# The first stage of a two-block transformer kernel: modulation by native fp32 products in column quarters, the norm's multiplications on another engine, five projections by parts, and filler products

## The chip, the cores and the metric

The kernel runs on one core of a Trainium2 chip. The metric is the device time of one execution in microseconds, the median of several executions. Lower is better. All work is in fp32; the inputs lie in the chip's memory when the clock starts.

## The reference, cut to what matters

Two transformer blocks over 512 tokens of 1024 channels run one after the other. The change lies in the first lines of block 1:

```python
m = silu(c) @ w_mod + b_mod                  # c: 1 x 1024, w_mod: 1024 x 6144
sh1, sc1, g1, sh2, sc2, g2 = split(m, 6)
mc = silu(c_ctx) @ w_mod + b_mod             # the same weights for the context
h = rms_norm(x, norm1_g) * (1 + sc1) + sh1       # x: 512 tokens x 1024
hc = rms_norm(ctx, norm1_g) * (1 + csc1) + csh1  # ctx: 256 tokens x 1024
# four mixers on h @ w_in and hc @ w_in: grouped attention, neighbourhood
# attention, a Fourier mix, and a 31-tap convolution; gates, w_out, experts
```

`rms_norm` divides each token by the root of the mean square over its 1024 channels. Nothing of `h @ w_in` can start before the shifts and scales of the modulation (`sh1`, `sc1`) and the norm of `x` are there.

## The kernel before, in words

All tensors lie transposed, channels on the partitions and tokens along the free axis: `x` is 8 chunks of 128 channels by 512 tokens. A product in fp32 is made of three products in a reduced fp32 type (`mm3`): each operand is split into a high and a low part (`h_hi`, `h_lo`; `whi`, `wlo`), and high times high, low times high and high times low are added up in a PSUM bank. The high part of a weight is a CAST on ScalarE (ACT), the low part a subtraction on VectorE (DVE). A weight that is not split is multiplied natively in fp32 (called whole in `_load`).

The program is written as threads (generators). While it is built, a rough clock of the engines (class `Clock`) picks which thread is traced next, and each engine then runs its instructions strictly in the traced order. Every instruction passes through the helper `Lane.call`, so nearly all rows of the profile carry line L320; instructions are told apart by their tiles. Weights come in loads of 512 KB on SP's queue (SyncE); a load waits until its tile in a ring is free, and what stands behind it on SP waits too.

The first stage (`mixers`) is:

- `silu_c` (line 706) makes silu of `c` and `c_ctx` (tile `csil`) and its split (`cparts`).
- `modulated` (771) makes the squares of `x` on ACT (`xsq`), adds the eight chunks on DVE (`xacc`), sums over the channels by four products of TensorE (PE) with ones, takes the power -0.5 on GpSimd (POOL, `xr`), spreads the result by four transposes, copies it out of PSUM (`xbc`) and multiplies the eight chunks of `x` by it on POOL.
- `jobs_mod` (727) and `mod_job` (734) make the modulation's 2048 columns for `sh1` and `sc1` in four groups of 512 columns: four loads of `w_mod` each (`mraw`), the first one native, the other three split (`mod_hi`, `mod_lo`). A product has 4 columns of `csil` or `cparts` as its stationary side and 512 columns of the weights as its moving side, so its result stands on 4 partitions. The group's sum is copied to SBUF (`m`), turned to the partitions by four small products (`pairs`), and gives a shift and a scale `A` for two chunks of `x`, the event `mod0` to `mod3`.
- `modulated_chunk` (791) makes `h_hi` and `h_lo` of one chunk from these, on ACT and DVE.
- `conv_first` (1010) multiplies the first 3 (`FIRST`) units of `w_in` at once, by pairs of chunks: as soon as a pair of chunks of `h` is there, 3 units by 6 products run. The convolution has 8 such units; `conv_job` does the others one after the other, 24 products each. `taps` then makes the 31 taps of four channel groups on DVE; a group needs two units.
- `zeros` clears a row in memory (`yg`) by DMA from a tile `ct` that POOL clears. On SP's queue these DMAs stand ahead of the tables of the Fourier mix (`ldft`).
- The context goes through `modulated` too (`hcsq`, `hcacc`, `hcr`, `ctx`), beside the first units.

Of the kernel before, what the change touches and what calls it, by code (L numbers as in the profile page):

```python
# [35 lines left out]
FIRST = 3  # L36
# [71 lines left out]
_HALF = np.concatenate([np.arange(0, 64, 2), np.arange(1, 64, 2)])  # L108

# the columns of w_mod by 128: shift and scale of each 256 channels, and the rest  # L110
# [92 lines left out]
def _span(ap):  # L203
    """the tile of an access pattern, and the range of its elements on a partition"""
    pairs = ap.ap
    row = pairs[0][0]
    lo = ap.offset % row if row > 0 else ap.offset
    hi = lo
    for s, n in pairs[1:]:
        d = s * (n - 1)  # L210
        if d < 0:
            lo += d
        else:
            hi += d
    return ap.tensor.name, lo, hi + 1


class Clock:
# [91 lines left out]
class Lane:  # L310
    """an engine, with what is traced on it noted on the clock"""
# [26 lines left out]
class Ring:  # L338
    """tiles that are taken and given back in any order"""
# [17 lines left out]

class Thread:
# [9 lines left out]
class Net:  # L368
    """The kernel. What it does is written as threads (generators), which yield the engine that their next
    instructions run on and what those wait for; `run` traces them in the order of a rough clock's times, the first  # L370
    in time first. Each engine runs its instructions in the order in which they are traced."""
# [199 lines left out]
    def proj(self, out, w, act, kt, n):  # L571
        """out[128 channels, n tokens] = the weights' columns by the activations"""
# [5 lines left out]
    def proj_t(self, out, w, act, t):  # L578
        """out[128 tokens of tile t, 256 channels]; w: the two halves of the contraction"""
# [7 lines left out]
    def split(self, hi, lo, src, *free):  # L587
        """hi + lo = src; then the rings' tiles in `free` are given back"""
# [7 lines left out]
    def evacuate(self, out, p, n):  # L596
        """a bank's first n columns into out"""
# [8 lines left out]
    def evacuated(self, ring, p, n):  # L606
        """a bank's first n columns, in a tile of the ring"""
# [8 lines left out]
    def rsqrt_mean(self, out, sums, n):  # L616
        """out = (sums / n + eps) ** -0.5"""
# [6 lines left out]
    def row_bcast(self, out_sb, colv, nt):  # L624
        """out_sb[128, nt * 128] = the [128 tokens, nt] column values, along the tokens on every row"""
# [8 lines left out]
    def square(self, acc, x, sq, first, scaled=None):  # L634
        """acc (+)= x ** 2, by a tile of the ring sq; scaled: also (f * x) ** 2, by f and its square"""
# [15 lines left out]
    def column_sums(self, r, acc, nt, n):  # L651
        """r[128 tokens, nt] = (mean over n channels of the squares in acc + eps) ** -0.5"""
# [7 lines left out]
    def sumsq(self, p, nt, k, x, sq):  # L660
        """columns of p: the sums over the 128 channels of chunk k of x ** 2, by tokens"""
        yield ACT, x, sq
        t = sq.take()
        self.nc.scalar.activation(t[:, :nt * 128], x, AF.Square)
# [6 lines left out]
    def rms(self, r, p, nt, nk):  # L671
        """r[128 tokens, nt] = (mean over the chunks' channels + eps) ** -0.5; the bank p is given back"""
# [6 lines left out]
    def square_last(self, x, sq, event):  # L679
        """a tile of the ring sq with x ** 2"""  # L680
# [6 lines left out]
    def column_sums2(self, r, acc, x, sq, event, nt, n):  # L687
        """r[128 tokens, nt] = (mean over n channels of the squares in acc, and of those of x, which the event gives,
        + eps) ** -0.5"""
# [16 lines left out]
    def silu_c(self):  # L706
        """silu(c) and silu(c_ctx), and their parts"""
        nc = self.nc
        self.csil = self.keep.tile([128, 8, 4], F32, name="csil")
        nc.gpsimd.memset(self.csil, 0.0)  # L710
        self.cparts = self.keep.tile([128, 8, 4], F32R, name="cparts")
        self.pairs = self.keep.tile([4, 2], F32, name="pairs")
# [5 lines left out]
        c = self.csil[:, :, :2]  # L718
# [4 lines left out]
        nc.vector.tensor_tensor(self.pairs, self.ident[:4, :2], self.ident[:4, 2:4], op=OP.add)  # L723
        yield from self.split(self.cparts[:, :, 0:2], self.cparts[:, :, 2:4], c)
        self.mark("cparts", self.cparts, c)

    def jobs_mod(self, a, after=None):
        if after:
            yield [], partial(self.hold, after)
        for g in range(2 * a, 2 * a + 2):  # L730
            for kq in range(4):
                yield [(self.T["wmod1"][g, kq], 2, 512, kq == 0)], partial(self.mod_job, g, kq)

    def mod_job(self, g, kq, w):
        """rows of the bank: the parts of c by the weights' columns"""
        nc = self.nc
        if kq == 0:
            yield PE, self.banks, "cparts"
            self.modp = self.banks.take()
        p = self.modp  # L740
        for k in range(2):
            for z, v in enumerate(w):
                c = self.csil if len(w) == 1 else self.cparts
                nc.tensor.matmul(p[:4, :], c[:, kq * 2 + k], v[:, k], start=kq + k + z == 0,
                                 stop=(kq, k, z) == (3, 1, len(w) - 1))
# [5 lines left out]
        nc.vector.tensor_copy(m, p[:4, :])  # L751
# [2424 lines left out]
```

## Time and profile before

| quantity | before |
|---|---|
| device time, three runs | 2464.28, 2461.07, 2462.39 us |
| median | 2462.39 us |
| span of the profiled execution | 2460.7 us |
| PE busy (products) | 2395.9 us, 97% |
| DVE busy | 1675.1 us, 68% |
| ACT busy | 1236.0 us, 50% |
| POOL busy | 160.3 us, 7% |
| idle time of PE | 64.8 us |

The profile lists the span of the profiled execution; its device time is not listed apart from those of the three runs. The span lies 1.7 us under their median. PE is the engine that sets the time nearly everywhere: of the 64.8 us in which it is idle, 11.3 are its wait for the first load of `w_mod` and 6.0 more fall into the first 50 us. The stage is read from the rows of its engines.

### The profile page before, as it was taken

Reading aid. Unit: us, or ns where it says so; the run is one execution under the profiler, and the core shown is the slowest. Engines: PE = TensorE matmul, PEld = TensorE weight load, DVE = VectorE, ACT = ScalarE, POOL = GpSimd, SP = SyncE. Lnnn points to the kernel's source line nnn. Section 1 sums busy time; section 2 is a strip of 40 time slices with the busy share of each in tenths; the row PEclk is TensorE's granted clock in tenths of the full one; section 3 lists DMA queues with packets and bytes.
Section 4 is the critical chain, followed back from the end, with each engine's and each line's share of the span. In section 5 each row is a group of like instructions: output and inputs, shape, how many; then the busy total and the mean of one; then the engine's idle time right before and its main releaser. Section 6 shows DMA issues by size and latency. Waiting matters only on the chain.

```text
span 2460.7 us, 33539 instructions
## 1 busy us (share of the span) xinstructions
PE 2395.9 (97%) x12332; PEld 2011.6 (82%) x12332; DVE 1675.1 (68%) x3144; ACT 1236.0 (50%) x2135; POOL 160.3 (7%) x179
## 2 busy tenths in 40 slices
PE   7999999999997999999999999999999999999998
PEld 3789788889886788887889888888888888888886
DVE  6997577788455989898998753444569976533443
ACT  4433466468342777775537743332443665432333
POOL 3100122100001110002000000000000000000000
PEclk9999999999997999999999999999999999999999
DMA  6223443521363998985121132222232112222221
GB/s 251 97 69 107 134 128 111 170 77 44 99 213 113 351 384 325 353 325 182 64 78 53 44 103 94 94 97 101 95 101 78 53 64 72 95 100 95 94 98 57
DMA packets 104907, 323.79 MB, mean 132 GB/s; under 512 B 12850, under 2 KB 19922, under 8 KB 104612
## 3 DMA queue, kind: packets, MB, share of 16 engines
q1 hardware_dynamic: 91284, 285.40, 33.0%
q0 software_dynamic: 8560, 25.01, 3.5%
q10 hardware_dynamic: 4896, 11.22, 1.2%
q8 instruction: 98, 1.61, 0.3%
q14 instruction: 69, 0.57, 0.1%
HBM read 308.45 MB, written 13.11 MB: 131 GB/s over the span
## 4 chain that ended last, share of the span: by engine, by line
PE 38%; issue 14%; DVE 1%; DMA 0%; ACT 0%; ACTq 0%; POOLq 0%; POOL 0%; DVEq 0%
PE bank L320 38%; DMA mraw<-yg,dest 0%; DVE wlo L320 0%; DVE G L320 0%; DVE cP L320 0%; DVE ym L320 0%; DVE mt L320 0%; DVE m L320 0%; ACTq L320 0%; DVE x L320 0%; DVE o L320 0%; ACT whi L320 0%; POOLq L3172 0%; POOL r L320 0%; DVE nm L320 0%
## 5 line engine op out<-in xcount | busy, mean ns | idle before, releaser
L320 ACT CAST whi<-wraw 128x1024 fp32r<-128x1024 f32 (+1 forms) x321 | 322.1, 1006 | 666.8 <-PE bank L320 633.2
L320 DVE TENSOR_TENSOR wlo<-wraw,whi 128x1024 fp32r<-128x1024 f32 (+1 forms) x321 | 375.4, 1173 | 155.6 <-ACT whi L320 154.8
L320 PE MATMUL bank<-g_hi,whi 128*128 128x512 f32 x992 | 395.9, 399 | 0.0
L320 PE MATMUL bank<-g_hi,wlo 128*128 128x512 f32 x992 | 387.3, 390 | 0.2
L320 PE MATMUL bank<-g_lo,whi 128*128 128x512 f32 x992 | 386.5, 390 | 0.0
L320 PEld LDWEIGHTS bank<-g_hi,wlo 128*128 128x128 f32 x992 | 186.2, 188 | 40.9 <-DVE wlo L320 1.1
L320 PE MATMUL bank<-h_hi,whi 128*128 128x512 f32 x528 | 216.9, 411 | 1.5 <-ACT whi L320 1.5
L320 PEld LDWEIGHTS bank<-g_hi,whi 128*128 128x128 f32 x992 | 186.5, 188 | 37.9 <-issue 1.9
L320 PEld LDWEIGHTS bank<-g_lo,whi 128*128 128x128 f32 x992 | 186.5, 188 | 37.1 <-issue 1.9
L320 PE MATMUL bank<-h_hi,wlo 128*128 128x512 f32 x528 | 209.3, 396 | 1.3 <-DVE wlo L320 1.3
L320 PE MATMUL bank<-h_lo,whi 128*128 128x512 f32 x528 | 208.6, 395 | 1.6 <-DVE h_lo L320 1.6
L320 PE MATMUL bank<-u_hi,whi 128*128 128x512 f32 x512 | 202.4, 395 | 0.0
L320 PE MATMUL bank<-u_hi,wlo 128*128 128x512 f32 x512 | 200.7, 392 | 0.0
L320 PE MATMUL bank<-u_lo,whi 128*128 128x512 f32 x512 | 198.8, 388 | 0.0
L320 DVE SCALAR_TENSOR_TENSOR mu<-bank,rbc 128x512 f32<-128x512 f32 x64 | 44.0, 691 | 161.0 <-PE bank L320 157.4
L320 ACT CAST whi<-mraw 128x1024 fp32r<-128x1024 f32 x101 | 105.7, 1050 | 55.0 <-PE bank L320 25.1
L320 DVE TENSOR_TENSOR wlo<-mraw,whi 128x1024 fp32r<-128x1024 f32 x101 | 121.0, 1218 | 16.5 <-ACT whi L320 14.5
L320 PEld LDWEIGHTS bank<-h_hi,wlo 128*128 128x128 f32 x528 | 100.6, 191 | 24.5 <-DVE wlo L320 2.5
L320 PEld LDWEIGHTS bank<-h_hi,whi 128*128 128x128 f32 x528 | 101.0, 191 | 21.3 <-ACT whi L320 1.9
L320 PEld LDWEIGHTS bank<-h_lo,whi 128*128 128x128 f32 x528 | 100.9, 191 | 19.5 <-DVE h_lo L320 2.1
L320 PEld LDWEIGHTS bank<-u_hi,wlo 128*128 128x128 f32 x512 | 96.1, 188 | 22.5
L320 PEld LDWEIGHTS bank<-u_lo,whi 128*128 128x128 f32 x512 | 96.1, 188 | 21.2
(539 smaller groups left out, 5017.7 us busy)
## 6 DMA issues: line engine op xcount, KB each, us to landing
mraw<-in_wgu SPq DMA_DIRECT2D x106, 512.0 KB
wraw<-in_win SPq DMA_DIRECT2D x102, 512.0 KB
wraw<-in_wdn SPq DMA_DIRECT2D x78, 512.0 KB
wraw<-in_wup SPq DMA_DIRECT2D x64, 512.0 KB
mraw<-in_wdn SPq DMA_DIRECT2D x50, 512.0 KB
mw<-in_wmod SPq DMA_DIRECT2D x64, 256.0 KB
wraw<-in_wout SPq DMA_DIRECT2D x24, 512.0 KB
wraw<-in_wgu SPq DMA_DIRECT2D x22, 512.0 KB
```

The lines of the kernel that those rows point to most:

```text
L320: r = f(*args, **kw)
```

## The change

The diff, without comments, cut to its core:

```diff
-FIRST = 3
+FIRST = 5
+class Both(Ring):
...
     def sumsq(self, p, nt, k, x, sq):
-        yield ACT, x, sq
+        e = self.lighter()
+        yield e, x, sq
         t = sq.take()
-        self.nc.scalar.activation(t[:, :nt * 128], x, AF.Square)
+        if e == ACT:
+            self.nc.scalar.activation(t[:, :nt * 128], x, AF.Square)
+        else:
+            self.nc.vector.tensor_tensor(t[:, :nt * 128], x, x, op=OP.mult)
         yield PE, t
         for j in range(nt):
             c = j * 8 + k
             self.nc.tensor.matmul(p[:, c:c + 1], t[:, j * 128:(j + 1) * 128], self.ones1, start=True, stop=True)
...
     def silu_c(self):
-        self.csil = self.keep.tile([128, 8, 4], F32, name="csil")
+        self.csil = self.keep.tile([128, 46], F32, name="csil")
-        self.cparts = self.keep.tile([128, 8, 4], F32R, name="cparts")
-        self.pairs = self.keep.tile([4, 2], F32, name="pairs")
+        self.pairs = self.keep.tile([128, 2], F32, name="pairs")
...
+    def warm(self):
+        yield PE, self.banks, self.ident
+        p = self.banks.take()
+        while "x7" not in self.events:
+            yield PE, self.ident
+            self.nc.tensor.matmul(p[:, :128], self.ident, self.ident, start=True, stop=True)
+        self.banks.drop(p)
-    def jobs_mod(self, a, after=None):
+    def jobs_mod(self, groups):
-                yield [(self.T["wmod1"][g, kq], 2, 512, kq == 0)], partial(self.mod_job, g, kq)
+                yield [(self.T["wmod1"][g, kq], 2, 512, True)], partial(self.mod_job, g, kq)
     def mod_job(self, g, kq, w):
         for k in range(2):
-            for z, v in enumerate(w):
-                c = self.csil if len(w) == 1 else self.cparts
-                nc.tensor.matmul(p[:4, :], c[:, kq * 2 + k], v[:, k], start=kq + k + z == 0,
-                                 stop=(kq, k, z) == (3, 1, len(w) - 1))
+            c = 2 * kq + k
+            q = 32 * (c % 4)
+            nc.tensor.matmul(p[q:q + 32, :], self.csil[:, 2 * c:2 * c + 32], w[0][:, k], start=c < 4, stop=c >= 4)
...
-        nc.vector.tensor_copy(m, p[:4, :])
+        nc.vector.tensor_copy(m, p)
...
     def modulated(self, pool, x, nt, v, hi, lo, name):
-        sq = self.ring(pool, 2, [128, n], F32, name + "sq")
-        acc = pool.tile([128, n], F32, name=name + "acc")
+        sq = self.ring(pool, 3, [128, n], F32, name + "sq")
+        yield PE, self.banks, x[:, 0]
+        p = self.banks.take()
         for k in range(8):
-            yield from self.square(acc, x[:, k], sq, k == 0)
+            yield from self.sumsq(p, nt, k, x[:, k], sq)
         r = self.keep.tile([128, nt], F32, name=name + "r")
-        yield from self.column_sums(r, acc, nt, 1024)
-        bc = pool.tile([128, n], F32, name=name + "bc")
-        yield from self.row_bcast(bc, r, nt)
-        for k in range(8):
-            yield POOL, bc
-            nc.gpsimd.tensor_tensor(x[:, k], x[:, k], bc, op=OP.mult)
+        yield from self.rms(r, p, nt, 8)
+        yield PE, self.banks, r
+        bc = self.banks.take()
+        for j in range(nt):
+            nc.tensor.transpose(bc[:, j * 128:(j + 1) * 128], r[:, j:j + 1].to_broadcast([128, 128]), self.ident)
         for k in range(8):
+            yield DVE, bc
+            nc.vector.tensor_tensor(x[:, k], x[:, k], bc[:, :n], op=OP.mult)
             self.spawn(self.modulated_chunk(k, x[:, k], v, hi[:, k], lo[:, k], f"{name}{k}"), 1, name)
...
     def mixers(self):
-            rings = self.ring(pool, 6, [128, 1024], F32, "mraw1"), self.pair_ring(pool, 3, [128, 1024], "mod1")
-            self.m512 = self.ring(pool, 2, [4, 512], F32, "m512")
+            raws = self.ring(pool, 6, [128, 1024], F32, "mraw1")
+            self.m512 = self.ring(pool, 2, [128, 512], F32, "m512")
...
-            self.stream(self.jobs_mod(0), 6, "mod_a", rings, prio=0)
-            self.stream(self.jobs0(), 2, "jobs0")
-            self.stream(self.jobs_mod(1, "jobs0 loaded"), 6, "mod_b", rings, prio=0)
+            self.spawn(self.warm(), 3, "warm", 0.3)
+            firsts = Both(self.pair_ring(pool, FIRST - 3, [128, 1024], "first"), self.his)
+            self.stream(self.jobs_mod((0,)), 8, "mod_a", (raws, None), prio=0)
+            self.stream(self.jobs0(), 2, "jobs0", (self.raws, firsts))
+            self.stream(self.jobs_mod((1, 2, 3)), 8, "mod_b", (raws, None), prio=0)
...
     def jobs0(self):
-        yield [], partial(self.hold, "mod_a loaded")
```

A modulation product now has 32 columns on its stationary side and writes one of the four quarters of a bank's partitions, by the chunk of the contraction; the small products with `pairs` add up the quarters as they turn them. All 16 loads of `w_mod` are taken natively, so the 12 CASTs and 12 subtractions of their splits go. The squares of `x` are made by ACT and DVE, whichever is lighter, and each chunk is summed over its channels by PE at once; the eight multiplications of `x` (and of `ctx`) are done by DVE straight from the PSUM bank. Five units of `w_in` (their parts in two rings that `Both` joins) are loaded ahead and multiplied by pairs of chunks. `warm` puts products of the identity with itself into PE's order wherever the rough clock sees PE idle, until the last chunk of `h` is there.

The traced order changes in the program's first part alone: with buffer numbers left out, PE's order is the same again behind about its first 970 instructions, DVE's behind its first 290 or so. The first place is PE ahead of the first product of `h`. (`bank` is a PSUM bank, `m` the copied sum of a group, `pairs` the small turning products, `ident` the filler.) Before, after the products of groups 0 and 1:

```order
L320 MATMUL bank_69<-mod_hi_138,cparts 4x512
L320 MATMUL bank_69<-mod_lo_141,cparts 4x512
L320 MATMUL bank_71<-pairs,m_143 128x2 x4
L320 MATMUL bank_72<-mraw_132,csil 4x512 x2
L320 MATMUL bank_73<-h_hi,whi_101 128x512
L320 MATMUL bank_73<-h_lo,whi_101 128x512
```

Now, from the last loads of group 3 on:

```order
L320 MATMUL bank_72<-mraw_132,csil 32x512 x2
L320 MATMUL bank_72<-mraw_133,csil 32x512 x2
L320 MATMUL bank_73<-pairs,m_136 128x2 x4
L320 MATMUL bank_67<-pairs,m_137 128x2 x4
L320 MATMUL bank_66<-ident 128x128 x5
L320 MATMUL bank_69<-pairs,m_136 128x2 x4
L320 MATMUL bank_66<-ident 128x128 x29
L320 MATMUL bank_68<-pairs,m_137 128x2 x4
L320 MATMUL bank_66<-ident 128x128 x13
L320 MATMUL bank_70<-h_hi,first_hi_161 128x512
```

The turning products of all four groups, those of group 0 too, moved behind the last product of group 3, 47 fillers stand among and behind them, and the first product of `h` moved behind all of these. From there on 120 products of five units follow, with the context's sums (16 products with ones) and its 2 transposes among them.

The second place is PE's start, which before began with the first load of `w_mod`. Now it begins with 16 fillers, and ends so, down to the first product of group 0 (`xsq` are squares of `x`, each summed by four products with ones):

```order
L320 MATMUL bank_67<-ones_82,xsq_160 128x1 x4
L320 MATMUL bank_66<-ident 128x128 x3
L320 MATMUL bank_67<-ones_82,xsq_158 128x1 x4
L320 MATMUL bank_67<-ones_82,xsq_159 128x1 x4
L320 MATMUL bank_66<-ident 128x128
L320 MATMUL bank_68<-mraw_130,csil 32x512 x2
```

In all 32 products with ones and 27 fillers (16, 3, 4, 3 and 1) now stand ahead of group 0's products; before, four products with ones stood behind the first of them. Another 20 fillers stand between the products of groups 0 and 1.

The third place is POOL. Before:

```order
L320 TENSOR_TENSOR xr<-ms,half 128x4
L320 TENSOR_TENSOR x<-x,xbc 128x512 x8
L320 DMA token<-in_k_token 128x4
L320 TENSOR_TENSOR hcr<-ms,half 128x2
L320 TENSOR_TENSOR ctx<-ctx,hcbc 128x256 x8
L320 MEMSET ct_147 1x512
```

Now:

```order
L320 TENSOR_TENSOR xr<-ms,half 128x4
L320 DMA token<-in_k_token 128x4
L320 TENSOR_TENSOR hcr<-ms,half 128x2
L320 MEMSET ct_142 1x512
```

The clearing of `ct`, for which SP's queue waits, no longer stands behind the eight multiplications of `ctx`.

## Rows read from the trace of the kernel before

**Rows 1.** The page: span, and busy time, share and instructions of each engine.

```profile
span 2460.7 us, 33539 instructions
PE 2395.9 (97%) x12332; PEld 2011.6 (82%) x12332; DVE 1675.1 (68%) x3144; ACT 1236.0 (50%) x2135; POOL 160.3 (7%) x179
```

**Rows 2.** Busy time by stretch (start:end, length, then each engine's), clock, DMA share, GB/s.

```profile
8.00:30.00 22.00, 16.11 (x52) 5.91 (x52) 16.12 (x18) 14.90 (x20) 11.22 (x7) 1.00 1.00 399
...
100.00:150.00 50.00, 50.00 (x288) 44.16 (x287) 46.33 (x80) 19.20 (x40) 0.00 (x0) 0.98 0.16 53
```

**Rows 3.** Timeline of PE (start, duration, instruction, idle time before): modulation, and the first unit.

```profile
11.26 3.57 PE L320 MATMUL bank<-mraw,csil 128*4 128x512 f32 x4 [11.26 <-DMA mraw<-in_wmod]
14.76 1.87 PE L320 MATMUL bank<-ones,xacc 128*128 128x1 f32 x8
21.85 1.88 PE L320 MATMUL bank<-mraw,csil 128*4 128x512 f32 x4
...
35.34 0.80 PE L320 MATMUL bank<-h_hi,whi 128*128 128x512 f32 x1
...
52.84 1.05 PE L320 MATMUL bank<-pairs,m 4*128 4x2 f32 x8
53.82 0.50 PE L320 MATMUL bank<-h_hi,whi 128*128 128x512 f32 x1
```

**Rows 4.** Timeline of PE: products of `h`, the context's sums, the 120th product of `h`.

```profile
63.80 0.39 PE L320 MATMUL bank<-h_hi,wlo 128*128 128x512 f32 x1
...
66.97 0.39 PE L320 MATMUL bank<-h_lo,whi 128*128 128x512 f32 x1
...
71.83 0.50 PE L320 MATMUL bank<-ones,hcacc 128*128 128x1 f32 x4
72.19 0.49 PE L320 MATMUL bank<-h_hi,whi 128*128 128x512 f32 x1
...
78.67 0.39 PE L320 MATMUL bank<-h_hi,wlo 128*128 128x512 f32 x1
```

**Rows 5.** Timelines of DVE and ACT: from the scale of group 2 to the last chunk.

```profile
54.13 0.16 DVE L320 SCALAR_TENSOR_TENSOR A<-mod,vecs 128x4 f32<-128x4 f32 x1
54.39 0.81 ACT L320 ACTIVATE h_hi<-x,mod,A 128x512 fp32r<-128x512 f32 x1 [5.30 <-DVE A L320]
56.88 0.81 ACT L320 ACTIVATE h_hi<-x,mod,A 128x512 fp32r<-128x512 f32 x1 [0.32 <-DVE A L320]
58.31 1.47 DVE L320 TENSOR_TENSOR h_lo<-x,h_hi 128x512 fp32r<-128x512 f32 x2
```

**Rows 6.** Timeline of POOL, and of SP's queue (time of issue).

```profile
20.73 15.97 POOL L320 TENSOR_TENSOR x<-x,xbc 128x512 f32<-128x512 f32 x8 [1.87 <-ACT xbc L320]
74.83 8.78 POOL L320 TENSOR_TENSOR ctx<-ctx,hcbc 128x256 f32<-128x256 f32 x8 [1.07 <-ACT hcbc L320]
83.56 0.52 POOL L320 MEMSET ct<- 1x512 f32 x1
84.11 0.57 SPq L320 DMA_DIRECT2D yg<-ct  x2
...
91.31 9.05 SPq L320 DMA_DIRECT2D wraw<-in_win  x6
```

**Rows 7.** Timeline of PE about the first unit of the Fourier mix.

```profile
94.99 0.39 PE L320 MATMUL bank<-h_hi,wlo 128*128 128x512 f32 x1
96.89 0.50 PE L320 MATMUL bank<-h_hi,whi 128*128 128x512 f32 x1 [1.51 <-ACT whi L320]
...
102.01 0.40 PE L320 MATMUL bank<-h_hi,whi 128*128 128x512 f32 x1
```

**Rows 8.** Groups on DVE (xcount, busy us, mean ns), 68.5 to 87.4 us, then 87.4 to 220.

```profile
L320 DVE SCALAR_TENSOR_TENSOR ca<-cz,vecs,ca 128x512 f32<-128x512 f32 x7 | 7.4, 1087 | 0.0
...
L320 DVE SCALAR_TENSOR_TENSOR ca<-cz,vecs,ca 128x512 f32<-128x512 f32 x113 | 78.8, 745 | 0.5
```

**Rows 9.** A group on DVE, 0 to 60 us.

```profile
L320 DVE TENSOR_TENSOR mod_lo<-mraw,mod_hi 128x1024 fp32r<-128x1024 f32 x12 | 15.9, 1354 | 2.4 <-ACT mod_hi L320 2.4
```

More of the change, by code (lines that the diff above doesn't have):

```diff
@@ L355, in ready, with __init__, take, drop @@
         return free[n - 1] + 0.15 if len(free) >= n else None
+class Both(Ring):
+    def __init__(self, *rings):
+        self.rings = rings
+    def take(self):
+        return min((r for r in self.rings if r.ready() is not None), key=lambda r: r.ready()).take()
+    def drop(self, *tiles):
+        for t in tiles:
+            next(r for r in self.rings if t.tensor.name in r.busy).drop(t)
+    def ready(self, n=1):
+        return min((r.ready() for r in self.rings if r.ready() is not None), default=None)
 class Thread:
@@ L717, in silu_c @@
         yield ACT, cv
-        c = self.csil[:, :, :2]
+        c = self.csil[:, :16].rearrange("p (k c) -> p k c", k=8)
         nc.scalar.activation(c, cv, AF.Tanh, scale=0.5)
@@ L722, in silu_c @@
         nc.vector.tensor_scalar(c, c, 0.5, None, op0=OP.mult)
-        nc.vector.tensor_tensor(self.pairs, self.ident[:4, :2], self.ident[:4, 2:4], op=OP.add)
-        yield from self.split(self.cparts[:, :, 0:2], self.cparts[:, :, 2:4], c)
-        self.mark("cparts", self.cparts, c)
-    def jobs_mod(self, a, after=None):
-        if after:
-            yield [], partial(self.hold, after)
-        for g in range(2 * a, 2 * a + 2):
+        nc.vector.tensor_reduce(self.pairs, self.ident.rearrange("p (q v) -> p v q", q=4)[:, :2], axis=AX.X, op=OP.add)
+        self.mark("csil", c, self.pairs)
+    def warm(self):
[6 more added lines that the diff above has]
+    def jobs_mod(self, groups):
+        for g in groups:
             for kq in range(4):
-                yield [(self.T["wmod1"][g, kq], 2, 512, kq == 0)], partial(self.mod_job, g, kq)
+                yield [(self.T["wmod1"][g, kq], 2, 512, True)], partial(self.mod_job, g, kq)
     def mod_job(self, g, kq, w):
@@ L737, in mod_job @@
         if kq == 0:
-            yield PE, self.banks, "cparts"
+            yield PE, self.banks, "csil"
             self.modp = self.banks.take()
@@ L774, in modulated @@
         n = nt * 128
-        sq = self.ring(pool, 2, [128, n], F32, name + "sq")
-        acc = pool.tile([128, n], F32, name=name + "acc")
+        sq = self.ring(pool, 3, [128, n], F32, name + "sq")
+        yield PE, self.banks, x[:, 0]
+        p = self.banks.take()
         for k in range(8):
-            yield from self.square(acc, x[:, k], sq, k == 0)
+            yield from self.sumsq(p, nt, k, x[:, k], sq)
         r = self.keep.tile([128, nt], F32, name=name + "r")
-        yield from self.column_sums(r, acc, nt, 1024)
-        bc = pool.tile([128, n], F32, name=name + "bc")
-        yield from self.row_bcast(bc, r, nt)
+        yield from self.rms(r, p, nt, 8)
[3 more added lines that the diff above has]
+            nc.tensor.transpose(bc[:, j * 128:(j + 1) * 128], r[:, j:j + 1].to_broadcast([128, 128]), self.ident)
         for k in range(8):
-            yield POOL, bc
-            nc.gpsimd.tensor_tensor(x[:, k], x[:, k], bc, op=OP.mult)
-        for k in range(8):
+            yield DVE, bc
+            nc.vector.tensor_tensor(x[:, k], x[:, k], bc[:, :n], op=OP.mult)
             self.spawn(self.modulated_chunk(k, x[:, k], v, hi[:, k], lo[:, k], f"{name}{k}"), 1, name)
+        self.banks.drop(bc)
         yield DVE, *(f"{name}{k}" for k in range(8))
@@ L819, in modulation_rest @@
                     yield DVE, w
-                    c = self.csil[:, k, 0:1]
+                    c = self.csil[:, 2 * k:2 * k + 1]
                     if k == 0:
```

## The prediction

> **What bounds the kernel now.** I read the page first, then the first 220 us by stretches, then the timelines of PE, DVE, ACT, POOL and SP's queue. PE is busy 2395.9 of 2460.7 us [rows 1], so a change counts where it moves PE's order or opens or closes one of its waits. The new order differs from the old one in the first part alone, and PE has no idle time from 100 to 150 us [rows 2], where DVE is busy for 46.33 of 50 too. So what the first hundred microseconds lose or gain is carried on to the end nearly unchanged, and I price that stretch. Two marks fix it before: the first product of `h` starts at 35.34 [rows 3], and the 120th, which is five units of 24, ends at 78.67 plus one interval of 0.227, at 78.9 [rows 4]. The interval comes from the 15 products from 63.80 to 66.97, 3.17 us for 14 intervals. Behind them PE stands still once more: from 94.99 to 102.01 only ten products start, which at 0.227 take 2.27 of 7.02 us, so 4.75 are lost [rows 7].
>
> **PE's start.** Before, PE begins with the first load at 11.26 and makes four sums. Now 32 sums and 27 fillers stand ahead of group 0. Four sums took 1.87 us at 14.76 [rows 3], 0.47 each; two took 0.36 at 71.83 [rows 4], 0.18 each. A native product of 512 columns is two records: two of them took 3.57 us at 11.26 and 1.88 at 21.85 [rows 3], which are the clock's levels of 1.2 and 2.4 GHz, near 1.75 and 0.9 us a product. A filler of 128 columns is a quarter of one, an estimate of 0.44 and 0.22. So sums and fillers take 5.8 + 5.9 = 11.7 us at the upper level and 15.0 + 11.9 = 26.9 at the lower. The 16 fillers at the front run while `x` is still on its way. The transfers move 399 GB/s [rows 2], 1.31 us for a load of 512 KB; `x` is the four loads before the one that released PE at 11.26, so its last part lands near 10. Group 0's products can start at 11.5 at the earliest and near 28 at the latest. I take 20, nearer to the lower clock, at which PE works so early in the rows of before.
>
> **The loads.** Fourteen loads go out without a wait; with the fifth at 11.26 and 1.31 each the fourteenth lands at 23.1. The other eleven wait on SP for tiles that PE's products free. If these come free in time, the last of the 25 lands at 11.26 + 20 x 1.31 = 37.5. With group 0 from 20 on, the first tiles come free near 22, which starves the transfers by some 4 us; I take 41.5 for the last, and with its two products P = 42.5 for the first turning products behind it.
>
> **The quarters.** No row shows products side by side in different quarters, so their price lies between 0.9 us each (one after the other, upper level) and a fourth, 0.22. I take 0.45: a product is two records, and the next quarter's first can stand beside the second. At 0.9 us for the two products of a load they keep up with 1.31. The Trainium skill, in "TensorE: Matmul & The Clock Gate", part 3, reports 2.38 times the speed for three such column tiles; by it the 32 products would take 32 x 0.9 / 2.38 = 12.1 us, an estimate, against the 14.4 that I use, and the sum would not change, since the loads come last.
>
> A switch between quarters and the full array may cost something. The nearest row is the step from two products with a 4-column stationary side at 11.26 to full ones at 14.76: 3.5 us for two products of 1.75, so under 0.1 us a switch, and I take nothing for the few that there are. The Trainium skill, in "TensorEngine Tiling (Array Packing)", key properties, says that a change of the tiling mode drains the engine; the row shows no drain that can be told from its rounding.
>
> **The turning products and the fillers.** All four groups' turning products now stand behind the last load's products, with 47 fillers, ahead of the first product of `h`. A set takes 0.98 us (52.84 to 53.82) [rows 3]. At the upper level this is 4 x 0.98 + 47 x 0.22 = 14.3 us on PE, so the first product of `h` would start at T = 42.5 + 14.3 = 56.8. The work beside it is a little shorter: from the first set's start 1.29 to the scale (52.84 to 54.13), 2.49 for each of the next two groups (54.39 to 56.88), 5.65 from the third group's scale to the last low part (54.13 to 58.31 + 1.47) [rows 3, 5], 11.9 in all. At the lower level the 47 would cost 10 us more. I take T = 57.
>
> **The five units.** 120 x 0.227 = 27.2 us, eight pairs of context sums at 0.36 are 2.9, two transposes, half a filler's price each, 0.2 to 0.4. That ends at T + 30.5 = 87.5, against 78.9: 8.6 us later. DVE and ACT are ahead by then.
>
> **What goes.** Twelve subtractions of 1354 ns and twelve CASTs beside them go [rows 9], and seven additions of squares for four squares on DVE. They gave PE waits only in the stretch that T replaces, so they count nothing beyond it. POOL's 15.97 and 8.78 us of multiplications go; DVE's eight and eight, near 0.69 and 0.42 us by size, stand where the loads are still waited for, or beside the five units. The clearing of `ct` was behind them at 83.56; `yg` at 84.11, the tables behind it and the next weights at 91.31 follow on SP's queue [rows 6], and those weights are what PE lacks from 95 to 102. Now `ct` is cleared right after the context's power, so these issues no longer wait for POOL while PE comes 8.6 us later. I take the whole 4.75 back; its ends are 0 and 4.75.
>
> **The sum.** 8.6 - 4.75 = 3.85 us later: 2462.39 + 3.85 = 2466.2. It is made against the profiled execution, whose span of 2460.7 lies 1.7 under the median; I carry that 1.7 along. Put shortly, the kernel loses T - 53.15, so no loss needs T = 53.15.
>
> **The rivals.**
> *Not slower.* The sums end by 12 to 14 us, the loads never starve, P is 37.5 + 0.9 = 38.4, and the fillers take half of my estimate, so that the work beside them (11.9) decides: T = 50.3, and 2462.4 - 2.85 = 2459.5. Under T = 53.15 it wins. For it: transfers are full from 8 to 30 us [rows 2] and nothing on SP waits for the first fourteen. Against: 43 instructions in PE's order ahead of group 0, each priced above.
> *The wait comes back.* The taps of the convolution begin only when all five units are through. Before, seven taps of 1087 ns and the set-up of two groups, about 10 us, were done by 87.4; these join the 113 of 745 ns behind it [rows 8], where DVE idles 3.67 in 50 us [rows 2], some 9 until 220. Low parts of weights queue behind taps, and PE waits again: the 4.75 stay lost, 2462.4 + 8.6 = 2471.0.
> *The quarters do nothing.* One after the other at the lower level, group 0 takes 8 x 1.75 = 14 us to 34, the other 24 at the upper level 21.6, so P is 55.6 and T 69.9: 16.8 us, 2479.2. No row speaks against it.
>
> **How the numbers follow.** A measurement of this kernel can tell about 0.2% from no change, 4.9 us. My forecast (T from 54 to 60, wait gone, +1 to +7) has 0.38, of which 0.22 lies within 4.9; not slower 0.26, of which 0.12 lies beyond 4.9 below, since T could go under 48.2 if PE's fillers and sums cost still less; the wait back 0.20; no quarters 0.16. So faster 0.12, same 0.14 + 0.22 = 0.36, slower 0.16 + 0.20 + 0.16 = 0.52. The range from 2457.5 to 2482.0 leaves out the quickest part of the second case and the lower clock throughout the fourth.
>
> **What would show it.** Group 0's first product near 20 us, the last load near 41, four sets of turning products behind each other from 42.5, the first product of `h` at 57, the five units' end near 87.5 with no gap inside, and no stop of PE at the first unit of the Fourier mix. Records of `mraw` products that overlap would show the quarters side by side. I am wrong if T is under 53, if the quarters' records follow each other at 0.43 us, or if PE waits for `wlo` between 90 and 220 us.

## The result and the profile after

The changed kernel takes 2475.89 us (2474.97 to 2477.07, four runs) against 2462.55 for the kernel before: a ratio of 1.0054, interval 1.0039 to 1.0068, 13.3 us slower. The span of its profiled execution is 2475.2, that of before 2460.7 [rows 1].

The page's first lines, after:

```profile
span 2475.2 us, 34009 instructions
PE 2420.2 (98%) x12604; PEld 2041.4 (82%) x12604; DVE 1658.2 (67%) x3143; ACT 1220.9 (49%) x2112; POOL 136.7 (6%) x163
```

PE is busy 24 us more, though the result needs no more work than before: its order has 94 fillers and 42 more products with ones (48 instead of 6), and in some stretches its products run at the lower clock. The stretches (busy time of PE, PEld, DVE, ACT, POOL; then PE's clock, DMA share, GB/s):

```profile
10.00:20.00 10.00, 10.00 (x55) 10.00 (x54) 1.38 (x2) 3.68 (x5) 0.00 (x0) 0.56 1.03 413
20.00:30.00 10.00, 10.00 (x53) 6.80 (x54) 3.44 (x7) 1.51 (x2) 2.63 (x2) 0.59 0.52 174
...
60.00:70.00 10.00, 10.00 (x56) 9.01 (x55) 2.90 (x8) 1.76 (x5) 0.34 (x1) 0.79 0.00 1
70.00:80.00 10.00, 10.00 (x41) 8.09 (x40) 7.08 (x20) 5.39 (x12) 0.86 (x2) 0.87 0.00 0
```

PE's timeline, which answers to [rows 3, 4] (start, duration, instruction, idle time before; two records are one native product):

```profile
1.34 5.27 PE L320 MATMUL bank<-ident 128*128 128x128 f32 x32 [1.34 <-POOL ident masks.py:199]
7.77 1.95 PE L320 MATMUL bank<-ones,xsq 128*128 128x1 f32 x16 [1.16 <-ACT xsq L320]
...
19.35 3.41 PE L320 MATMUL bank<-ones,xsq 128*128 128x1 f32 x16
22.62 0.78 PE L320 MATMUL bank<-ident 128*128 128x128 f32 x2
23.33 3.64 PE L320 MATMUL bank<-mraw,csil 128*32 128x512 f32 x16
...
27.81 4.85 PE L320 MATMUL bank<-ident 128*128 128x128 f32 x40
32.59 2.84 PE L320 MATMUL bank<-mraw,csil 128*32 128x512 f32 x24
38.96 4.92 PE L320 MATMUL bank<-mraw,csil 128*32 128x512 f32 x16 [3.53 <-DMA mraw<-in_wmod]
...
45.39 1.05 PE L320 MATMUL bank<-mraw,csil 128*32 128x512 f32 x4 [0.23 <-DMA mraw<-in_wmod]
46.37 1.95 PE L320 MATMUL bank<-pairs,m 128*128 128x2 f32 x16
...
50.19 6.72 PE L320 MATMUL bank<-ident 128*128 128x128 f32 x58
...
57.56 3.15 PE L320 MATMUL bank<-ident 128*128 128x128 f32 x26
60.46 0.48 PE L320 MATMUL bank<-h_hi,first_hi 128*128 128x512 f32 x1
...
64.67 1.50 PE L320 MATMUL bank<-ones,hcsq 128*128 128x1 f32 x12
...
94.65 0.39 PE L320 MATMUL bank<-h_hi,wlo 128*128 128x512 f32 x1
```

Eight sums (two records each) took 1.95 us at 7.77 and 3.41 at 19.35: the clock had fallen while PE worked without a pause (0.56 from 10 to 20). The first product of `h` starts at 60.46 instead of 35.34, the 120th at 94.65 instead of 78.67: 25.1 and 16.0 us later. The stop at the Fourier mix [rows 7] is gone: products run through from 110.29 to 111.93 with at most 0.28 between two starts, and the weights that were missing are issued at 99.96 behind a `ct` cleared at 70.34 [rows 6]. That leaves 11.3 us, and so it stays to 265 us. Then something opens that the kernel before does not have. SP's queue, DVE and PE there, after:

```profile
257.79 15.11 SPq L320 DMA_DIRECT2D nv<-nvd  x18
272.94 0.47 SPq L320 DMA_DIRECT2D mw<-in_wmod  x1
273.46 0.42 SPq L320 DMA_DIRECT2D wraw<-in_wbranch  x1
...
279.07 0.35 DVE L320 TENSOR_SCALAR macc<-mw,csil 128x256 f32<-128x256 f32 x1 [16.05 <-DMA mw<-in_wmod]
...
279.86 1.22 DVE L320 TENSOR_TENSOR wlo<-wraw,whi 128x1024 fp32r<-128x1024 f32 x1
...
281.13 0.80 PE L320 MATMUL bank<-h_hi,wlo 128*128 128x512 f32 x1 [8.25 <-DVE wlo L320]
```

and before:

```profile
229.13 0.40 SPq L320 DMA_DIRECT2D mw<-in_wmod  x1
245.06 0.33 SPq L320 DMA_DIRECT2D wraw<-in_wbranch  x1
246.43 15.79 SPq L320 DMA_DIRECT2D nv<-nvd  x18
```

Before, the first load of the second modulation part (`mw`) and one load of `w_branch` stood ahead of 18 small transfers of the neighbourhood values, now they stand behind them. `macc` on DVE waits for `mw`, the low part of a weight waits behind `macc`, and PE waits 8.25 us for that. Counted by the products of `h` in order, the delay grows from 11.1 us at the 528th to 21.1 at the 576th and falls to 16.4 at the 624th, where the kernel before waits 4.4 us for `macc` and the changed one 1.8; at the last product it is 14.4.

### The profile page after: what moved, and what is told of

Same layout as the page of the kernel before. It is cut to its first block, busy times and chain, and to the rows that moved or that the text cites. A ratio compares the mean times of both kernels' runs of the same rounds, so it can differ in the third digit from the quotient of the medians.

```text
span 2475.2 us, 34009 instructions
## 1 busy us (share of the span) xinstructions
PE 2420.2 (98%) x12604; PEld 2041.4 (82%) x12604; DVE 1658.2 (67%) x3143; ACT 1220.9 (49%) x2112; POOL 136.7 (6%) x163
## 4 chain that ended last, share of the span: by engine, by line
PE 75%; issue 15%; DVE 5%; DMA 3%; ACT 1%; SPq 1%; POOL 0%; another core or an unknown queue 0%; ACTq 0%; POOLq 0%; DVEq 0%
PE bank L320 75%; DMA nbm<-in_rpb 1%; DVE wlo L320 1%; SPq L320 1%; ACT nP L320 0%; DMA mraw<-in_wgu 0%; DMA mraw<-in_wmod 0%; DVE m L320 0%; DVE macc L320 0%; DMA mraw<-yg,dest 0%; DVE nqs L320 0%; DVE pairs L320 0%; DVE G L320 0%; DMA wraw<-in_wbranch 0%
## 5 line engine op out<-in xcount | busy, mean ns | idle before, releaser
L320 ACT CAST whi<-wraw 128x1024 fp32r<-128x1024 f32 (+1 forms) x319 | 320.1, 1006 | 681.8 <-PE bank L320 630.8
L320 DVE TENSOR_TENSOR wlo<-wraw,whi 128x1024 fp32r<-128x1024 f32 (+1 forms) x319 | 370.8, 1167 | 148.4 <-ACT whi L320 147.8
L320 PE MATMUL bank<-g_hi,whi 128*128 128x512 f32 x992 | 395.8, 399 | 0.0
L320 PE MATMUL bank<-g_hi,wlo 128*128 128x512 f32 x992 | 387.2, 390 | 0.2
L320 PE MATMUL bank<-g_lo,whi 128*128 128x512 f32 x992 | 386.4, 389 | 0.0
L320 PEld LDWEIGHTS bank<-g_hi,wlo 128*128 128x128 f32 x992 | 186.2, 188 | 40.9 <-DVE wlo L320 1.1
L320 PEld LDWEIGHTS bank<-g_hi,whi 128*128 128x128 f32 x992 | 186.5, 188 | 38.0 <-issue 1.9
L320 PEld LDWEIGHTS bank<-g_lo,whi 128*128 128x128 f32 x992 | 186.5, 188 | 36.9 <-issue 1.9
L320 PE MATMUL bank<-h_hi,wlo 128*128 128x512 f32 x512 | 201.9, 394 | 8.3 <-DVE wlo L320 8.2
L320 PE MATMUL bank<-h_hi,whi 128*128 128x512 f32 x512 | 209.0, 408 | 0.0
L320 PE MATMUL bank<-u_hi,whi 128*128 128x512 f32 x512 | 202.3, 395 | 0.0
L320 PE MATMUL bank<-h_lo,whi 128*128 128x512 f32 x512 | 201.0, 393 | 0.0
L320 PE MATMUL bank<-u_hi,wlo 128*128 128x512 f32 x512 | 200.7, 392 | 0.0
L320 PE MATMUL bank<-u_lo,whi 128*128 128x512 f32 x512 | 198.8, 388 | 0.0
L320 DVE SCALAR_TENSOR_TENSOR mu<-bank,rbc 128x512 f32<-128x512 f32 x64 | 44.1, 692 | 161.0 <-PE bank L320 157.4
L320 ACT CAST whi<-mraw 128x1024 fp32r<-128x1024 f32 x101 | 105.7, 1050 | 56.6 <-PE bank L320 30.1
L320 DVE TENSOR_TENSOR wlo<-mraw,whi 128x1024 fp32r<-128x1024 f32 x101 | 121.2, 1221 | 16.9 <-ACT whi L320 16.5
L320 PEld LDWEIGHTS bank<-h_hi,wlo 128*128 128x128 f32 x512 | 96.9, 189 | 30.7 <-DVE wlo L320 9.7
L320 PEld LDWEIGHTS bank<-u_hi,wlo 128*128 128x128 f32 x512 | 96.1, 188 | 22.5
L320 PEld LDWEIGHTS bank<-u_lo,whi 128*128 128x128 f32 x512 | 96.1, 188 | 21.2
L320 PEld LDWEIGHTS bank<-u_hi,whi 128*128 128x128 f32 x512 | 96.3, 188 | 19.0
L320 PEld LDWEIGHTS bank<-h_hi,whi 128*128 128x128 f32 x512 | 97.4, 190 | 16.6 <-issue 0.2
```

Source lines behind the costliest of these rows:

```text
L320: r = f(*args, **kw)
```

## The experiments

Three questions were open: whether the fillers cost their place or pay with the clock, what the new wait at 273 us is worth, and which parts of the change are good in a better order. Each time is a median, with the ratio to the runs of the kernel before on the same chip and its interval. Experiments 1 to 4 ran on one chip, 5 to 7 and the changed kernel again on a second, 8 to 10 on a third; the kernel before took 2461.64, 2461.05 and 2462.44 us there, so differences across these groups carry up to 1.4 us of that. In some kernels two more lines ahead of the helper turn L320 into L322. The columns at the right are the starts of the first and the 120th product of `h` in the profile.

| kernel | us | ratio (interval) | 1st | 120th |
|---|---|---|---|---|
| before | 2462.55 | | 35.3 | 78.7 |
| changed | 2475.89 | 1.0054 (1.0039 to 1.0068) | 60.5 | 94.7 |
| changed, again | 2478.86 | 1.0066 (1.0053 to 1.0080) | 60.6 | 94.8 |
| 1: SP's order of before | 2475.24 | 1.0045 (1.0031 to 1.0059) | 65.7 | 99.9 |
| 2: fillers out, all else in place | 2476.42 | 1.0060 (1.0046 to 1.0074) | 53.1 | 92.8 |
| 3: no fillers, ordered anew | 2466.46 | 1.0018 (1.0009 to 1.0027) | 46.0 | 80.5 |
| 4: ordered by a clock that knows the quarters | 2449.86 | 0.9950 (0.9937 to 0.9964) | 36.7 | 69.9 |
| 5: 3 with SP's order of before | 2463.82 | 1.0009 (1.0000 to 1.0018) | 45.8 | 79.8 |
| 6: 4 with sums chunk by chunk | 2463.44 | 1.0006 (0.9997 to 1.0015) | 43.0 | 82.6 |
| 7: 4 with all products in one quarter | 2461.91 | 0.9999 (0.9990 to 1.0008) | 45.5 | 83.2 |
| 8: 4 with the norm on POOL | 2456.94 | 0.9980 (0.9971 to 0.9988) | 40.6 | 73.9 |
| 9: 4 with three units by parts | 2456.23 | 0.9977 (0.9968 to 0.9986) | 29.4 | 70.5 |
| 10: 4 with the fillers | 2468.50 | 1.0029 (1.0017 to 1.0041) | 61.8 | 89.6 |

**1. SP's order of before.** Only the two loads move; no other row of any engine does.

```diff
     def modulation_rest(self, ws, accs):
                 nc.sync.dma_start(w, self.T["wmod2"][u, h // 2][:, h % 2 * 2:h % 2 * 2 + 2])
+                self.mark("mw0")
...
     def _load(self, w, issued, raws, his):
+        if "mw0" in self.events:
+            self.mark("wb0")
...
     def na_values(self):
-            yield SP, f"nvd{c // 2}", self.nvr
+            yield SP, f"nvd{c // 2}", self.nvr, "wb0"
```

> The changed kernel, with one edit: the 18 transfers of the neighbourhood values stand behind the first load of the second modulation part and one load of w_branch on SP's queue, as they did before the change; nothing else moves on any engine. Theory (the change's late loss of some 5 us sits at that queue: macc waits for its load, a low part of a weight waits behind macc on VectorE, TensorE waits 8.2 us for it): that wait goes, the 4.4 us wait for macc of the kernel before comes back in part, and the time falls by 3 to 4 us, to 2472 to 2473. Rival (the wait is due to TensorE's own lateness, which only shows there): no change, 2475 to 2476.5.

The median, 2475.24, lies in the rival's band, but it does not tell, with five times from 2469.47 to 2481.13. The trace does. PE's only long wait there is that of before, and none is for `wlo`:

```profile
PE bank L320 <- DVE macc L320: 5.3, 1, 5.3
```

From the 528th to the 624th product of `h` the delay against the kernel before grows by 0.8 us, where the changed kernel's grew by 5.3. The profiled execution, the slowest of the five, does not show the gain in its time: though its first stage has the changed kernel's order, it started `h` at 65.7 instead of 60.5. Why the median did not fall is not shown, as the other four were not profiled. The stretch from 40 to 60 us, first of the changed kernel, then of this one:

```profile
40.00:60.00 20.00, 19.48 (x146) 14.44 (x143) 8.85 (x21) 8.25 (x12) 0.00 (x0) 0.95 0.54 209
```

```profile
40.00:60.00 20.00, 18.39 (x98) 12.60 (x99) 7.66 (x18) 6.41 (x9) 0.00 (x0) 0.74 0.60 231
```

The first turning products came 2.0 us later here (48.39 against 46.37), and with a clock of 0.74 instead of 0.95 the same instructions from there to the first product of `h` took 17.3 us instead of 14.1.

**5. The same on a steadier first stage** (experiment 3's kernel with the edit of 1).

> The third experiment (no fillers, ordered anew) with the order on SP's queue of the first one. Theory (the neighbourhood values ahead of macc's first load cost TensorE 8 us and give 4 back later): no wait for a low part of a weight near 265, a wait of 4 to 5 us for macc, and 4 to 5 us less than the third experiment, 2461 to 2463. Rival: within 1.5 us of it, 2465 to 2468.

2463.82 against 2466.46, 2.6 us less, between theory and rival by the time; counted from the kernel before on each chip it is 2.1 us, and the intervals overlap, so the times alone do not show it. In the trace the delay from the 528th to the 624th product grows by 2.2 us instead of 5.1, with no wait for `wlo` and 5.7 us for `macc`. So the order on SP's queue is the cause of the late loss: with it alone changed, PE's wait for `wlo` is gone in both pairs of traces. It was worth 3 us here and 4.5 in the changed kernel up to 700 us, not the 8 of the wait alone. Behind that, both traces with the order of before lose some of it at a fall of the clock that their partners lack (0.89 from 720 to 735 us here and 0.91 from 735 to 755 in experiment 1, where the partners have 1.00).

**The changed kernel again.**

> The changed kernel again, unedited. In its first profile the first product of h started at 60.5 us; in the first experiment, with the same order of that stage, at 65.7, and its five times spread over 11.7 us. Theory (the clock's level in the first 60 us falls out differently from execution to execution, and the order of that stage makes the time hang on it): the five times spread over 6 us or more, the median lies at 2472 to 2478, and the first product of h starts somewhere between 57 and 66. Rival (one bad draw): the times lie within 3 us and the first product of h is at 60 to 61.

Five times from 2473.83 to 2481.53, the first product of `h` at 60.6, the median of 2478.86 just above the theory's band. The spread is as wide as the theory said, but the kernel before spread from 2457.14 to 2465.61 over 27 runs, so a greater sensitivity of the changed kernel is not shown; experiment 1's profile alone shows an execution with another clock.

**2. Fillers out, all else in place.**

```diff
         while "x7" not in self.events:
             yield PE, self.ident
-            self.nc.tensor.matmul(p[:, :128], self.ident, self.ident, start=True, stop=True)
+            self.clk.note(PE, "matmul", (p[:, :128], self.ident, self.ident), {})
```

> The changed kernel without its 94 filler products; every other instruction stands where it stood on every engine. Theory (the fillers cost their place in TensorE's order: 27 ahead of group 0, 47 ahead of the first product of h): the first product of h comes near 55 instead of 60.5, bound by the scales and the parts of h, and the time falls by 4 to 7 us, to 2469 to 2472. Rival (the fillers keep the clock at its upper level and pay for themselves): sums, modulation products and the first products of h run at the lower level, the first product of h comes at 59 or later, and the time is 2474 or more.

Both sides were half right. The first product of `h` came 7.4 us earlier, at 53.1, so the fillers' places cost that much. But the time is no better, because PE then ran at the lower clock, behind a stretch of products that waited for their loads and a wait of 5.35 us for a copied sum:

```profile
53.10 0.77 PE L320 MATMUL bank<-h_hi,first_hi 128*128 128x512 f32 x1
53.67 0.63 PE L320 MATMUL bank<-h_lo,first_hi 128*128 128x512 f32 x1
54.10 0.63 PE L320 MATMUL bank<-h_hi,first_lo 128*128 128x512 f32 x1
```

```profile
50.00:60.00 10.00, 8.63 (x30) 7.74 (x31) 4.91 (x10) 3.91 (x8) 0.00 (x0) 0.50 0.31 105
60.00:70.00 10.00, 10.00 (x36) 8.66 (x35) 1.49 (x5) 0.42 (x1) 1.20 (x2) 0.50 0.01 3
```

Products of `h` follow each other at 0.43 us instead of 0.23, and of the 7.4 us 1.8 are left at the 120th. In this order the fillers pay for their places, no more. Of the places, those up to the first turning products cost 4.1 us: these start at 42.25 here,

```profile
42.25 1.95 PE L320 MATMUL bank<-pairs,m 128*128 128x2 f32 x16
```

and at 46.37 with them.

**3. No fillers, ordered anew.** The one line that starts the thread `warm` goes.

> The changed kernel without the thread of fillers, so that the rough clock orders TensorE anew (turning products of group 3 now stand behind the first products of h). Theory (order, not clock, sets the first product of h): it starts near 44, the five units end at 76 to 79, and with the late loss on SP's queue still there the time is 2458 to 2464, below the changed kernel by 12 us or more and about that of before. Rival (clock): 2470 or more.

2466.46: 9.4 us under the changed kernel, not the 12 of the theory, and a little above its band. The first product of `h` starts at 46.0, the 120th at 80.5 against 78.7 before; the stop at the Fourier mix stays away, and what is lost in the end is the late loss (from 2.9 us ahead at the 528th product to 2.2 behind at the 624th).

**4. Ordered by a clock that knows the quarters.**

```diff
             elif ins[0].dtype != F32R or n < 256:
                 n = max(4 * n, 200)
+                if outs[0].partition_size() == 32:
+                    n //= 4
...
-            self.spawn(self.warm(), 3, "warm", 0.3)
...
     def modulated(self, pool, x, nt, v, hi, lo, name):
-            yield from self.sumsq(p, nt, k, x[:, k], sq)
-        yield from self.rms(r, p, nt, 8)
+            yield from self.square(acc, x[:, k], sq, k == 0)
+        yield from self.column_sums(r, acc, nt, 1024)
```

with SP's order of experiment 1.

> The changed kernel without fillers, with the squares added on VectorE before four sums as in the kernel before (for x and for the context), with the rough clock told that products in quarters take a fourth of their time, and with SP's order of the first experiment. What remains of the change: native modulation products in quarters, no splits, norm multiplications on VectorE, five units by parts. Theory (what was lost lay in the order and the sums, not in quarters, splits or the norm): turning products stand right behind their groups, the first product of h starts at 33 to 37, the five units end at 69 to 72, and the time is 2449 to 2457, below both kernels. Rival (the wait at the first unit of the Fourier mix comes back, or low parts of weights queue behind the taps on VectorE): 2458 to 2464.

2449.86, ratio 0.9950 (0.9937 to 0.9964): below both kernels, within the theory's band, 11.8 us under the 2461.64 of before on the same chip and 26 under the changed one. Four things differ from the changed kernel at once (fillers, sums, the price of quarters, SP's order); the experiments below take some of them apart. PE's timeline:

```profile
10.94 1.92 PE L322 MATMUL bank<-mraw,csil 128*32 128x512 f32 x4 [10.94 <-DMA mraw<-in_wmod]
13.69 1.86 PE L322 MATMUL bank<-ones,xacc 128*128 128x1 f32 x8 [0.83 <-DVE xacc L322]
...
24.01 1.87 PE L322 MATMUL bank<-pairs,m 128*128 128x2 f32 x8 [4.04 <-DVE m L322]
25.81 4.70 PE L322 MATMUL bank<-mraw,csil 128*32 128x512 f32 x20
32.14 1.05 PE L322 MATMUL bank<-pairs,m 128*128 128x2 f32 x8 [1.63 <-DVE m L322]
...
36.65 0.50 PE L322 MATMUL bank<-h_hi,first_hi 128*128 128x512 f32 x1
```

Group 0 is turned at 24.0 instead of 46.4, and groups 2 and 3 are multiplied between the first units' products. The 120th product comes 8.8 us before that of the old kernel, and the stop at the Fourier mix stays away: 13.5 us ahead from there on.

**6, 7, 8, 9 and 10. Parts of the change, each put back or taken out of 4.** Edits: `sumsq` and `rms` again for `square` and `column_sums`; `q = 0` with `start=c == 0, stop=c == 7`; the norm's multiplications by `nc.gpsimd` from an SBUF copy; `FIRST = 3`; `warm` again. Experiment 7 has the order of 4 on every engine, 8 has it on PE and SP; in 6, 9 and 10 the rough clock orders PE anew, so each prices an edit together with the order that follows from it. Counted from the kernel before on their own chips, the five lie 14.2, 12.6, 6.3, 5.6 and 17.8 us above 4.

> The fourth experiment, but with the squares summed chunk by chunk by TensorE as in the changed kernel (32 sums of 128x1 for x and 16 for the context in place of 4 and 2, no additions on VectorE). Theory (these sums hold TensorE at the lower clock and stand ahead of group 0, and lower the clock among the first products of h): the first product of h at 42 to 46 instead of 36.7, the five units' end 9 to 12 us later, 2457 to 2462. Rival (they run in time that TensorE waits for loads anyway): 2452 or less.

2463.44, 13.6 us more than 4 and a little above the theory's band. The sums of `x` run at the pace of the lower clock from end to end (0.216 us a record; at 19.35 in the changed kernel it was 0.20), and group 0 waits behind them:

```profile
7.80 13.81 PE L322 MATMUL bank<-ones,xsq 128*128 128x1 f32 x64 [7.80 <-ACT xsq L322]
21.54 1.93 PE L322 MATMUL bank<-mraw,csil 128*32 128x512 f32 x8
...
30.08 1.87 PE L322 MATMUL bank<-pairs,m 128*128 128x2 f32 x8 [3.70 <-DVE m L322]
```

The first product of `h` is 6.3 us late against 4, and the 120th 12.7.

Experiment 6 is also experiment 5 with the price of the quarters added, on the same chip. In 5 the turning products of group 0 stand behind all groups:

```profile
42.77 1.95 PE L320 MATMUL bank<-pairs,m 128*128 128x2 f32 x16
```

With the price they come at 30.08, right behind their group. So the price is what moves them. But the time is the same, 2463.44 against 2463.82, the first product of `h` 2.8 us earlier and the 120th 2.8 later: with the sums in place, the price alone gains nothing. What it brings once the sums are gone no run here shows, since none has the sums gone and the old price.

> The fourth experiment, but with all modulation products in the first quarter of the array's columns, in the same order. Theory (quarters run side by side, four at a time, and are worth what one product after the other costs beyond the pace of the loads): two products take 1.7 us at the upper level and 3.4 at the lower against 1.3 for a load, the first product of h comes 3 to 9 us later, and the time is 2453 to 2460. Rival (the loads set the pace either way): within 1.5 us of 2449.9.

2461.91, 12.1 us more, in the same order and above the theory's band. Where 4 makes 10 products in 4.70 us at 25.81, this one needs 11.68, and the first product of `h` comes 8.8 us later:

```profile
27.61 11.68 PE L322 MATMUL bank<-mraw,csil 128*32 128x512 f32 x20
```

> The fourth experiment, but with the norm's multiplications (x and context) on GpSimd again, from a copy in SBUF, as in the kernel before. Theory (moving them pays: 16 us on GpSimd against some 5.5 on VectorE ahead of the parts of h, and VectorE no longer slowed beside them): 2452 to 2457. Rival (they lie beside the loads on either engine): 2449 to 2451.

2456.94, 7.1 us more, as the theory said; in the profiles 3.9 of it is there by 80 us and 4.9 in the spans. POOL's 11.9 us of multiplications slow DVE beside them (a low part of a weight takes 2.29 us instead of 1.21), and PE waits for the copied group:

```profile
35.22 1.87 PE L322 MATMUL bank<-pairs,m 128*128 128x2 f32 x8 [7.84 <-DVE m L322]
```

> The fourth experiment, but with three units by parts instead of five. Theory (two fewer loads of w_in ahead of the last modulation loads, and the first convolution groups finish earlier, while TensorE still finds enough work): 2444 to 2448. Rival (five units fill TensorE while the last scales come): 2451 to 2455.

2456.23, 6.4 us more than with five units and above both bands. `h` starts at 29.4, 7 us earlier, but at the 120th product of `h` it is 0.6 us behind: in the first stage the two are nearly even, so the rival is not shown either. The rest of the loss opens later, where the orders of PE and SP differ too: at the same products PE is some 4 us behind from 800 to 1100 us and 9 behind from 1150 on, after a fall of the clock that experiment 4 does not have (1120 to 1140 us, this one, then experiment 4):

```profile
1120.00:1140.00 20.00, 16.19 (x72) 13.04 (x73) 12.97 (x18) 4.40 (x6) 0.86 (x1) 0.83 0.45 156
```

```profile
1120.00:1140.00 20.00, 18.25 (x109) 15.72 (x110) 16.18 (x24) 9.05 (x14) 0.87 (x2) 1.00 0.34 110
```

What two more units by parts are worth stays open.

> The fourth experiment, but with the thread of fillers again. Theory (their places ahead of the turning products and the first product of h cost more than the clock they hold): the first product of h near 50, 2457 to 2463. Rival (with everything else in a good order they only fill gaps and hold the clock): 2450 or less.

2468.50, 18.6 us more, beyond the theory's band: 80 records of fillers run ahead of the first product of `w_mod`, others between the products of a group, 306 in all. PE waits for nothing from 1.34 to 100 us, and the first product of `h` moves from 36.7 to 61.8. The clock does hold (1.00 from 10 to 90 us), and the five units take 27.9 us from the first to the 120th start, against 33.3 in 4, where other products stand among them; the places still cost more.

## Why the prediction was right, and where its terms were off

It forecast a slower kernel, 3.85 us, and the time came out 13.3 us slower, in its range but in the upper part. Its main case reached from 1 to 7 us only; the range goes as far as 2482.0 for the sake of the rival without quarters (2479.2), which was false, so that the time lies in it is in part luck. None of the three signs of being wrong came: the first product of `h` is not under 53 us, the quarters' records start four at a time, and PE waits for no `wlo` between 90 and 220 us. By its steps:

- *The turning products and the fillers* were right: 14.3 us from the first turning product to the first product of `h` were forecast, 14.1 came (46.37 to 60.46).
- *PE's start* was mis-sized. I took 20 us for group 0's first product, and it started at 23.33: sums and fillers ran at the lower clock for most of the time from 10 us on (0.56 from 10 to 20). The first reloads came late with it. The 20 fillers between groups 0 and 1 had no price in my sum at all: they took 4.78 us (27.81 to 32.59), six loads of `w_mod` are issued only from 33.68 on behind them (from 26.27 in experiment 2), and PE then stood still 3.53. So P was 46.4 instead of 42.5, and T 60.5 instead of 57; without fillers, in experiment 2, P was 42.25. Early in a profile the level is to be read from durations: [rows 2] has a clock of 1.00 from 8 to 30 us, though the products at 11.26 take 1.75 us each.
- *The quarters* were worth more than I took. Sixteen records took 3.64 us at 23.33; in experiment 7 four records in one quarter took 3.60 us at 11.24. Both are at the pace of the lower clock, so eight products ran in the time of two: four quarters side by side, 0.45 us a product where I had 0.45 for the upper level. The rival that the quarters do nothing was false; experiment 7 prices it at 12 us in a good order. The Trainium skill, in "TensorE: Matmul & The Clock Gate", part 3, has 2.38 times for three tiles; the trace shows close to four times for four.
- *The switches* of the array cost little, if anything: the 16 records start in four rounds 0.85 us apart, the last at 25.90, and the full transposes start 1.0 us later, at 26.90, so at most some 0.15 us is the switch's. The Trainium skill, in "TensorEngine Tiling (Array Packing)", key properties, says that a change of the tiling mode drains the engine; a drain here is no longer than that.
- *The five units* were mis-sized. I took T + 30.5; it was 34.4, with the clock down behind the context's sums (0.79 and 0.87 from 60 to 80 us). I had priced these sums by their own time alone. That the sums are the cause is likely but not shown: the clock fell among or behind them in the changed kernel, its repeat and experiments 1 and 6, and did not in experiment 10, which has 2 in place of 16, but neither did it in 3 and 5, which have all 16.
- *What goes* was right in size: 16.0 us of delay became 11.3, the 4.7 that I took back. The reason I gave is not shown. The tables of the Fourier mix no longer wait for `ct` on SP's queue; they wait 23.3 us there for `wlo` instead. And in experiment 8, with the multiplications on POOL again, the stop is gone too (4.8 us ahead of the kernel before at the 120th product of `h`, 9.2 at the 200th). Which edit closes it stays open.
- *The order behind the first part* was the step that failed. I said that what the first hundred microseconds lose is carried on nearly unchanged. SP's order changed at 258 us as well, by two rows, and that cost 3 us net (11.3 to 14.4). The part on the change looks at PE's and DVE's order behind the first part, and not at SP's. (PE's and DVE's records differ once more, from 805 to 834 us; the delay does not grow there, 14.2 us ahead of it and 13.2 behind.) My rival of the wait that comes back named its kind, a low part of a weight late on DVE, but not its place: taps had nothing to do with it.

With these, 3.85 + 3.5 (T) + 3.9 (the units) + 3.1 (SP) makes 14.35, against 14.4 in the profiles.

Why the planner put the turning products last can be told from its cost: it took a product in a quarter for a whole one, so in its view PE, and not the loads, was the limit. Told the true price, it puts them right behind their groups (experiments 5 and 6). That order alone did not make the kernel faster; that the fillers and the sums had to go is shown by experiments 10 and 6.

## What to carry to other kernels

Where a planner sets the order, an edit moves other instructions too: tell the planner the price of a new instruction, but measure what the new order is worth, since here it gained nothing as long as the sums stood ahead of it. Compare the orders of all queues, DMA queues too, over the whole program and not where the change was made. Filler products on an in-order engine are paid for with every instruction behind them: give them only a place where the engine would truly wait. And spread a sum so that few tiny products are left on TensorE: seven additions on an engine with time to spare and 4 products were better than 32 products (with the context's 2 against 16, 13.6 us in experiment 6).

## What had not been expected of the hardware

PE can be busy all the time and still have its clock lowered: from 10 to 20 us it was busy 10.00 of 10.00 us, with sums of one column and some fillers, at a clock of 0.56; in experiment 6, 64 records of such sums without a gap took 13.81 us, 0.216 each, where [rows 4] has four in 0.36, 0.09 each. Four native products of 32 columns in different quarters run in the time of one (16 records in 3.64 us against 4 in one quarter in 3.60). And the same order of the same instructions can start `h` at 60.5 or 65.7 us, with another granted clock on the way (0.95 or 0.74 from 40 to 60 us).
